# PSUM banks at sub-layer boundaries, the place of a modulation's pieces, and a shift of the weight buffers in a two-layer trunk on one core

## Chip, core and metric

The kernel runs on one core of one Trainium2 chip. The metric is the device time of one execution in microseconds. Three executions of the kernel before give a median of 1439.07 us (1438.82 to 1439.69). The engines that matter are TensorE (PE, whose weight loads are shown as PEld), VectorE (DVE), ScalarE (ACT), GpSimd (POOL) and SyncE (SP), which issues the loads of the weights.

## The reference

Two layers of a trunk of width 1024 work on 128 context tokens and 256 latent tokens. Every layer is a feed-forward network with SwiGLU, a token mixer, and another feed-forward network. Each of these six sub-layers normalises its input, scales and shifts it by vectors that come from the conditioning, and gates its output before it is added to the stream:

```python
def swiglu(h, w1, w2):
    g, u = jnp.split(h @ w1, 2, axis=-1)
    return (jax.nn.silu(g) * u) @ w2

def modulate_norm(x, g, shift, scale):
    return rms_norm(x, g) * (1.0 + scale[:, None, :]) + shift[:, None, :]
```

The mixer of the even layer is neighbourhood attention beside a gated short convolution; that of the odd layer is a pooling mixer beside grouped-query attention with rotary positions. Shift, scale and gate of each sub-layer are products of SiLU(cond) with a matrix of 1024 x 1024 each, for two conditions (context and latent). All of it is in fp32.

## The kernel before

The 384 tokens are three tiles of 128: tile 0 is context, tiles 1 and 2 are latent. The residual stream `x` stays in SBUF. A product in fp32 is made of three matmuls (`mm3`, L443 to L445): both operands are split into a high and a low part, and high x high, low x high and high x low are added in PSUM. `xh` and `xl` are the parts of the current sub-layer's normalised and modulated input, transposed. The weights come in 1 MB pieces through four `raw` buffers, loaded by SP in the order of one list (`plan`, L1309); each piece has two halves, and each half is split by ACT (cast to `whi`, L152) and DVE (subtraction to `wlo`, L155) into one of three pairs of buffers, or into special ones (`macc`, `th`, `g`).

Beside the matmuls, DVE works out the modulation vectors of later sub-layers. A modulation matrix is four pieces of work (L229): a multiply and reduce of 128 x 1024 with `csB`, the SiLU of the conditions broadcast over partitions, which GpSimd loads (L203). The product goes to a bf16 scratch `junkv` that nobody reads. `emit_pieces` puts them between other work of DVE. `spread` (L1301) says where the matrices stand among a sub-layer's weights on SP's list.

The change touches the boundary between two sub-layers. The old sub-layer's last products are accumulated tile after tile, in PSUM banks 2 and 3, 4 and 5, 6 and 7 for tiles 0, 1 and 2. While TensorE is still at work on later tiles, the earlier ones are gated, added to `x`, normalised (`xn`), transposed on TensorE into PSUM and modulated out of PSUM into `xtmp` by DVE (L414) and ACT (L416), then cast to `xh` (ACT, L429) and subtracted to `xl` (DVE, L430). For tile 2 there is nothing of the old sub-layer left to hide this. `rest(early, late)` (L541) therefore lets the new sub-layer begin on tiles 0 and 1 (`early`), puts tile 2's transposes and modulation between, and comes back to the new sub-layer's first weights for tile 2 alone (`late`). In the feed-forward network `run_t2` (L656) multiplies tile 2 with the first two units, into `pn`; `fold` (L672) transposes the finished product and splits it. In the mixers `moving_first` (L1017) does the same, with `early` looping over token tiles and, in `moving`, over the `rows` of a half (2 in the even mixer, 1 in the odd one).

Up to this point the instructions are in the order in which the code writes them. The rest of the even mixer is ordered by a scheduler. There, `q`'s products in `psB0` and `psB1` are taken from PSUM by DVE (L1080) and ACT (L1081), then attention runs between the projections.

## Time and profile before

| | |
|---|---|
| median of three runs | 1439.07 us |
| the profiled execution | 1439.5 us |
| its span | 1437.6 us |
| TensorE busy | 1417.9 us, 99% |
| DVE busy | 1021.9 us, 71% |
| ACT busy | 614.6 us, 43% |

The durations that follow are those of the one profiled execution; its span is the time from the first to the last instruction. In a timeline a row is one instruction or a run of like ones, with its start, its duration, its engine and its line of the code; in brackets stands how long the engine had been idle before, and what ended that.

### The profile page before, as it was taken

How to read it: one execution, taken by the hardware profiler on the slowest of the kernel's cores; microseconds unless marked ns; L12 is line 12 of the kernel's file. 1: busy time of each engine (PE TensorE's matmuls, PEld its weight loads, DVE VectorE, ACT ScalarE, POOL GpSimd, SP SyncE). 2: the span in 40 equal slices, each digit the busy share in tenths (PEclk: the TensorE clock that was granted, in tenths of full speed). 3: DMA queues.
4: the chain of work that ended last, by engine and by line, in shares of the span. 5: the costliest groups of instructions: out<-in, count | busy, mean ns of one | idle time of the engine just before them, and what ended most of it. 6: DMA issues, size and time to landing. Idle time of an engine off the chain costs nothing.

```text
span 1437.6 us, 19880 instructions
## 1 busy us (share of the span) xinstructions
PE 1417.9 (99%) x7747; PEld 1299.1 (90%) x7747; DVE 1021.9 (71%) x1798; ACT 614.6 (43%) x1051; POOL 29.0 (2%) x54
## 2 busy tenths in 40 slices
PE   8999999999999999999999999999999999999998
PEld 6999998879888999999889999988886899999886
DVE  5688868578997677986855889787678755555333
ACT  5533332463545633333355333323657653333232
POOL 0000000020000000000000000000100000000000
PEclk9999999999999999999999999999999999999999
DMA  9556556626545246655734566566350234444331
GB/s 371 208 212 253 202 209 224 245 104 235 200 146 195 97 169 230 237 205 182 280 124 150 202 219 249 186 226 249 108 200 30 118 118 148 165 155 176 122 113 44
DMA packets 38959, 262.59 MB, mean 183 GB/s; under 512 B 4816, under 2 KB 4976, under 8 KB 8784
## 3 DMA queue, kind: packets, MB, share of 16 engines
q1 hardware_dynamic: 35424, 243.29, 46.2%
q0 software_dynamic: 3440, 18.02, 3.4%
q8 instruction: 61, 1.00, 0.3%
q14 instruction: 34, 0.28, 0.1%
HBM read 259.01 MB, written 2.29 MB: 182 GB/s over the span
## 4 chain that ended last, share of the span: by engine, by line
PE 93%; ACT 3%; DVE 3%; DMA 1%; issue 1%; DVEq 0%; SPq 0%; ACTq 0%
PE psB L443 29%; PE psB L444 29%; PE psB L445 29%; PE psB L391 2%; PE psB L938 1%; PE psB L979 1%; ACT xtmp L416 1%; DMA csB<-crows 1%; ACT junk L331 1%; ACT xh L429 1%; PE psB L785 0%; DVE xtmp L414 0%; ACT whi L152 0%; DVE wlo L155 0%; ACT L617 0%
## 5 line engine op out<-in xcount | busy, mean ns | idle before, releaser
L443 PE MATMUL psB<-xh,whi 128*128 128x384 f32 (+1 forms) x1536 | 519.5, 338 | 2.2 <-ACT qz L1081 2.0
L444 PE MATMUL psB<-xl,whi 128*128 128x384 f32 (+1 forms) x1536 | 514.7, 335 | 0.2 <-DVE xl L430 0.2
L445 PE MATMUL psB<-xh,wlo 128*128 128x384 f32 (+1 forms) x1536 | 514.2, 335 | 0.0
L155 DVE TENSOR_TENSOR wlo<-raw,whi 128x1024 fp32r<-128x1024 f32 (+2 forms) x286 | 336.4, 1185 | 121.8 <-ACT whi L152 120.0
L152 ACT CAST whi<-raw 128x1024 fp32r<-128x1024 f32 (+1 forms) x275 | 285.7, 1045 | 309.7 <-PE psB L444 147.7
L229 DVE CUSTOM_DVE_ANT_0 junkv<-raw,csB,mbT 128x1024 bf16<-128x1024 f32 x256 | 327.9, 1281 | 9.8 <-DMA csB<-crows 5.0
L443 PEld LDWEIGHTS psB<-xh,whi 128*128 128x128 f32 x1536 | 288.5, 188 | 7.0 <-ACT qz L1081 2.3
L444 PEld LDWEIGHTS psB<-xl,whi 128*128 128x128 f32 x1536 | 288.7, 188 | 1.8 <-DVE xl L430 0.9
L445 PEld LDWEIGHTS psB<-xh,wlo 128*128 128x128 f32 x1536 | 288.7, 188 | 0.4 <-issue 0.4
L443 PE MATMUL psB<-whi,g 128*128 128x512 f32 x384 | 149.9, 390 | 0.0
L445 PE MATMUL psB<-whi,g 128*128 128x512 f32 x384 | 149.5, 389 | 0.0
L444 PE MATMUL psB<-wlo,g 128*128 128x512 f32 x384 | 149.4, 389 | 0.0
L429 ACT CAST g<-gt 128x384 fp32r<-128x384 f32 (+1 forms) x84 | 42.5, 506 | 196.7 <-DVE gt L619 196.7
L619 DVE TENSOR_TENSOR gt<-psB,sil 128x384 f32<-128x384 f32 (+1 forms) x88 | 48.1, 547 | 90.1 <-PE psB L445 81.8
L443 PEld LDWEIGHTS psB<-whi,g 128*128 128x128 f32 x384 | 72.1, 188 | 15.1
L445 PEld LDWEIGHTS psB<-whi,g 128*128 128x128 f32 x384 | 72.1, 188 | 15.1
L444 PEld LDWEIGHTS psB<-wlo,g 128*128 128x128 f32 x384 | 72.1, 188 | 14.6
L617 ACT ACTIVATE sil<-psB 128x384 f32<-128x384 f32 (+1 forms) x88 | 42.7, 485 | 90.5 <-PE psB L445 90.4
L430 DVE TENSOR_TENSOR g<-gt,g 128x384 fp32r<-128x384 f32 (+1 forms) x84 | 46.1, 549 | 48.1 <-ACT g L429 48.1
L443 PE MATMUL psB<-g,g 128*128 128x512 f32 x120 | 47.0, 391 | 0.0
L445 PE MATMUL psB<-g,g 128*128 128x512 f32 x120 | 46.8, 390 | 0.0
L444 PE MATMUL psB<-g,g 128*128 128x512 f32 x120 | 46.7, 389 | 0.0
(227 smaller groups left out, 1410.9 us busy)
## 6 DMA issues: line engine op xcount, KB each, us to landing
raw<-in_ffn_w SPq DMA_DIRECT2D x129, 1024.0 KB, 4.9
raw<-in_mod_w SPq DMA_DIRECT2D x64, 1024.0 KB, 4.9
raw<-in_ev_in SPq DMA_DIRECT2D x10, 1024.0 KB, 6.2
m<-in_mod_first SPq DMA_DIRECT2D x8, 1024.0 KB, 13.0
gate<-gscr POOLq DMA_DIRECT2D x6, 1024.0 KB, 4.9
csB<-crows POOLq DMA_DIRECT2D x4, 1024.0 KB, 7.5
raw<-in_ev_out SPq DMA_DIRECT2D x4, 1024.0 KB, 4.9
raw<-in_od_out SPq DMA_DIRECT2D x4, 1024.0 KB, 4.8
```

The costliest lines, as they stand in the source:

```text
L152: nc.scalar.copy(hi, src)
L155: sub = lambda hi=hi[:, c], lo=lo[:, c], src=src[:, c]: nc.vector.tensor_tensor(lo, src, hi.bitcast(F32), ALU.subtract)
L229: nc.vector.tensor_tensor_reduce(junk, self.raw[i][0][:, kk * D : (kk + 1) * D], self.csB[:, c, :], 1.0, self.mbT[:, s, kind, k : k + 1], ...
L331: self.nc.scalar.activation(junk, srcs[h], AF.Square, scale=1.0 / 32.0, accum_out=ss[:, h : h + 1])
L391: self.nc.tensor.transpose(out, src, self.ident)
L429: self.nc.scalar.copy(hi, src)
L430: sub = lambda: self.nc.vector.tensor_tensor(lo, src, hi.bitcast(F32), ALU.subtract)
L443: nc.tensor.matmul(out, ah, bh, start=first, stop=False)
L444: nc.tensor.matmul(out, ah, bl, start=False, stop=False)
L445: nc.tensor.matmul(out, al, bh, start=False, stop=last)
L617: nc.scalar.activation(sil[:, :n], pg[:, :n], AF.Silu)
L619: nc.vector.tensor_tensor(gt[:, :n], pu[:, :n], sil[:, :n], ALU.mult)
```

## The change

Six things change.

1. Tile 2's transposes are put into four banks, two 128-column transposes each (4, 5, 2, 3; at the odd mixer 4, 5, 6, 7), in place of two banks with four each. DVE modulates the first and third bank, ACT the second and fourth.
2. In the feed-forward networks `pn` lies in banks 4 and 3 (before 2 and 0), and the folded product's transpose in 2 and 1 (before 4 and 1).
3. In the odd mixer tile 1's accumulators lie in banks 2 and 3 (before 6 and 7); `ups` and the transposes of queries and keys that follow change banks with them.
4. In `moving_first` the loop over `kk` stands outside that over the token tiles; the transposes stand between the first and the second `kk`. With one row, as in the odd mixer, the order is the old one.
5. In the even mixer the modulation matrices begin one place later on SP's list, and the source hands out the pieces only after the third projection tile.
6. The constant `one` takes 1 column in place of 25, and `junkv` 192 bf16 elements more. Behind `one` stand `xh` and others, 96 bytes lower; behind `junkv` stand the weight buffers, 288 bytes higher. Weight buffers and `xh` are 384 bytes further apart.

```diff
--- before.py
+++ after.py
@@ -66,7 +66,7 @@
         self.cc = cc
         self.ident = const("ident", [P, P])
         make_identity(nc, self.ident)
-        self.one = const("one", [P, 25])[:, 0:1]
+        self.one = const("one", [P, 1])
         nc.vector.memset(self.one, 1.0)
         self.xh = self.cp.tile([P, KC, TOK], F32R, tag="xh", name="xh")
         self.xl = self.cp.tile([P, KC, TOK], F32R, tag="xl", name="xl")
@@ -225,9 +225,9 @@
                     if u == 0:
                         self.mod_res = self.mod_vec(kind)
                 k = 2 * u + kk
-                junk = self.cp.tile([P, D], BF16, tag="junkv", name=self.name("junkv"))
+                junk = self.cp.tile([P, D + 192], BF16, tag="junkv", name=self.name("junkv"))
                 nc.vector.tensor_tensor_reduce(
-                    junk, self.raw[i][0][:, kk * D : (kk + 1) * D], self.csB[:, c, :], 1.0,
+                    junk[:, :D], self.raw[i][0][:, kk * D : (kk + 1) * D], self.csB[:, c, :], 1.0,
                     self.mbT[:, s, kind, k : k + 1], ALU.mult, ALU.add, self.mod_res[:, c, k : k + 1])
                 if kk == c == 1:
                     del self.raw[i]
@@ -392,8 +392,9 @@
 
     def transpose_x(self, xn, banks):
         tp = [self.psum(b) for b in banks]
+        n = KC // len(tp)
         for k in range(KC):
-            self.transpose(tp[k // 4][:, (k % 4) * P : (k % 4 + 1) * P], xn[:, k * P : (k + 1) * P])
+            self.transpose(tp[k // n][:, (k % n) * P : (k % n + 1) * P], xn[:, k * P : (k + 1) * P])
         return tp
 
     def evac_steps(self, t, tp, s):
@@ -408,8 +409,9 @@
                 for j in range(2):
                     c = 2 * e + j
                     k = 4 * q + c
-                    src, scale, shift = (tp[q][:, c * P : (c + 1) * P], self.scale[s][:, cond, k : k + 1],
-                                         self.shift[s][:, cond, k : k + 1])
+                    n = KC // len(tp)
+                    src, scale, shift = (tp[k // n][:, (k % n) * P : (k % n + 1) * P],
+                                         self.scale[s][:, cond, k : k + 1], self.shift[s][:, cond, k : k + 1])
                     if e == 0:
                         nc.vector.tensor_scalar(st[q, e][:, j, :], src, scale, shift, op0=ALU.mult, op1=ALU.add)
                     else:
@@ -559,7 +561,8 @@
             for f in subs[1 + odd :]:
                 f()
             evac = []
-            transposes = lambda: evac.append(self.evac_steps(2, self.transpose_x(xn2, (4, 5)), s + 1))
+            banks = (4, 5, 6, 7) if odd else (4, 5, 2, 3)
+            transposes = lambda: evac.append(self.evac_steps(2, self.transpose_x(xn2, banks), s + 1))
             early(0)
             finish = early(1)
             if odd:
@@ -656,7 +659,7 @@
             def run_t2(n):
                 u, h = divmod(n, 2)
                 if h == 0:
-                    pn[u] = self.psum((2, 0)[u])
+                    pn[u] = self.psum((4, 3)[u])
                 for kk in range(4):
                     k = 4 * h + kk
                     c = slice(kk * 256, kk * 256 + 256)
@@ -670,7 +673,7 @@
                 return None
 
             def fold(u, gn):
-                tp = self.psum((4, 1)[u])
+                tp = self.psum((2, 1)[u])
                 self.transpose(tp[:, 0:P], gn[:, 0:P])
                 gh, gl = g_of(u)
                 self.split(gh[:, t2], gl[:, t2], tp[:, 0:P])
@@ -1005,9 +1008,9 @@
         es.close()
         return nxt
 
-    def moving(self, ps, key, h, w, rows, width, t, blocks):
-
-        for kk in range(rows):
+    def moving(self, ps, key, h, w, rows, width, t, blocks, kks=None):
+
+        for kk in range(rows) if kks is None else kks:
             k = (2 * key[1] + h) * rows + kk
             for b, (c0, c1) in enumerate(blocks):
                 c = slice(kk * width + c0, kk * width + c1)
@@ -1023,10 +1026,11 @@
         def early(n, between=None):
             k, h = halves[n]
             ws.append(self.half(k, h, ahead=0, hold=True))
-            for t in range(2):
-                if t == 1 and between:
+            for kk in range(rows):
+                if kk == 1 and between:
                     between()
-                self.moving(ps, k, h, ws[-1], rows, width, t, blocks)
+                for t in range(2):
+                    self.moving(ps, k, h, ws[-1], rows, width, t, blocks, (kk,))
 
         def late():
             ps[2] = [self.psum(b) for b in banks[2]]
@@ -1146,7 +1150,8 @@
                 ps = self.proj_tile(key, h, n % 2, step)
                 n += 1
                 evac[kind](j, ps)
-                self.emit_pieces(pieces, 2)
+                if n > 3:
+                    self.emit_pieces(pieces, 2)
         while pieces:
             self.emit_pieces(pieces, 1)
         for _ in att:
@@ -1174,7 +1179,7 @@
         nc.gpsimd.dma_start(rope, io["rope"])
         tabs = mp.tile([P, 2, 2, 2, 64], F32, tag="tabs", name="tabs")
         units = [k for k in p1 if k[0] == "od_qkv"]
-        acc = self.moving_first(units, 1, 768, [(0, 512), (512, 768)], [(0, 1), (6, 7), (4, 5)], rest)
+        acc = self.moving_first(units, 1, 768, [(0, 512), (512, 768)], [(0, 1), (2, 3), (4, 5)], rest)
         for a in range(2):
             for b in range(2):
                 nc.vector.tensor_tensor(tabs[:, a, :, b, :], rope[:, :, b, :],
@@ -1219,12 +1224,12 @@
             return raw
 
         def qk_transpose(t, raw):
-            tp = self.psum((0, 6, 4)[t])
+            tp = self.psum((0, 2, 4)[t])
             for i in range(4):
                 self.transpose(tp[:, i * P : (i + 1) * P],
                                raw[:, 2 * i : 2 * i + 2, :].rearrange("p h d -> p (h d)"))
             nc.scalar.copy(qT[:, :, t * P : (t + 1) * P], tp.rearrange("p (i q) -> p i q", i=4))
-            tk = self.psum((1, 7, 5)[t])
+            tk = self.psum((1, 3, 5)[t])
             self.transpose(tk[:, 0:P], raw[:, 8:10, :].rearrange("p h d -> p (h d)"))
             c0 = 384 if t == 0 else (t - 1) * P
             nc.vector.tensor_copy(kz[0:64, 0, c0 : c0 + P], tk[0:64, 0:P])
@@ -1233,7 +1238,7 @@
         nc.gpsimd.dma_start(pm, io["pool_m"])
         nc.gpsimd.dma_start(pw, io["pool_w"])
         nc.gpsimd.dma_start(psc, io["pool_scale"])
-        ups = [[self.psum(2)], [self.psum(3)], None]
+        ups = [[self.psum(6)], [self.psum(7)], None]
         uc = [(k, h) for k in p1 if k[0] == "od_uc" for h in range(2)]
         raws = {}
         for n, (k, h) in enumerate(uc):
@@ -1323,7 +1328,7 @@
             b2 = [("od_out", i) for i in range(4)]
         n, n1 = MOD_PLAN[s]
         ext, mods = mods[:n], mods[n:]
-        b1 = spread(b1, ext[:n1], 3 if j == 1 else 5, len(b1))
+        b1 = spread(b1, ext[:n1], 4 if j == 1 else 5, len(b1))
         phases.append((b1, spread(b2, ext[n1:], 0, 7)))
     return phases, [k for p1, p2 in phases for k in p1 + p2]
 
```

TensorE's order at the boundary into the even mixer, before (`psB0` and `psB1` are the accumulators of tiles 0 and 1, `whi_496` and `wlo_497` the last half of the first weights, `psB4` and `psB5` hold the transposes of tile 2):

```order
L443 MATMUL psB0_482_2737<-whi_496_2777,xh_92 128x512
L444 MATMUL psB0_482_2737<-wlo_497_2778,xh_92 128x512
L445 MATMUL psB0_482_2737<-whi_496_2777,xl_93 128x512
L443 MATMUL psB0_482_2737<-whi_496_2777,xh_92 128x512
L444 MATMUL psB0_482_2737<-wlo_497_2778,xh_92 128x512
L445 MATMUL psB0_482_2737<-whi_496_2777,xl_93 128x512
L391 MATMUL psB4_506_2832<-ident_85,xn_505_2798 128x128 x4
L391 MATMUL psB5_507_2833<-ident_85,xn_505_2798 128x128 x4
L443 MATMUL psB1_483_2738<-whi_496_2777,xh_92 128x512
L444 MATMUL psB1_483_2738<-wlo_497_2778,xh_92 128x512
```

and after:

```order
L445 MATMUL psB0_482_2737<-whi_496_2777,xh_92 128x512
L446 MATMUL psB0_482_2737<-wlo_497_2778,xh_92 128x512
L447 MATMUL psB0_482_2737<-whi_496_2777,xl_93 128x512
L445 MATMUL psB1_483_2738<-whi_496_2777,xh_92 128x512
L446 MATMUL psB1_483_2738<-wlo_497_2778,xh_92 128x512
L447 MATMUL psB1_483_2738<-whi_496_2777,xl_93 128x512
L391 MATMUL psB4_506_2832<-ident_85,xn_505_2798 128x128 x2
L391 MATMUL psB5_507_2833<-ident_85,xn_505_2798 128x128 x2
L391 MATMUL psB2_508_2834<-ident_85,xn_505_2798 128x128 x2
L391 MATMUL psB3_509_2835<-ident_85,xn_505_2798 128x128 x2
L445 MATMUL psB0_482_2737<-whi_496_2777,xh_92 128x512
L446 MATMUL psB0_482_2737<-wlo_497_2778,xh_92 128x512
```

The second `kk` of tile 0, which needs the second half of `wlo`, has moved behind the transposes, and those have four banks.

TensorE's order in sub-layer 2, from the first two weights' products for tile 2 to the third's, before:

```order
L445 MATMUL psB2_921_4627<-macc_834_4228,xl_93 128x256
L443 MATMUL psB2_921_4627<-macc_834_4228,xh_92 128x256
L444 MATMUL psB2_921_4627<-macc_834_4228,xh_92 128x256
L445 MATMUL psB2_921_4627<-macc_834_4228,xl_93 128x256
L443 MATMUL psB0_925_4659<-whi_896_4484,xh_92 128x256
L444 MATMUL psB0_925_4659<-wlo_897_4485,xh_92 128x256
```

and after:

```order
L447 MATMUL psB4_925_4631<-macc_836_4230,xl_93 128x256
L445 MATMUL psB4_925_4631<-macc_836_4230,xh_92 128x256
L446 MATMUL psB4_925_4631<-macc_836_4230,xh_92 128x256
L447 MATMUL psB4_925_4631<-macc_836_4230,xl_93 128x256
L445 MATMUL psB3_929_4663<-whi_898_4486,xh_92 128x256
L446 MATMUL psB3_929_4663<-wlo_899_4487,xh_92 128x256
```

The order is the same; the second accumulator of tile 2 is bank 3 in place of bank 0, and the first one bank 4 in place of bank 2.

DVE's order in the even mixer, from the first copy of `v` to the first `q`, before (L1076 copies `v`, L229 are the modulation's pieces, L155 is a weight's low part, L1080 takes `q` out of `psB0`):

```order
L1076 COPY v_2729<-psB0_482_2737 128x512
L229 ISA junkv_534_3026,mv_533_3025<-raw_429_2471,csB_522_2928,mbT_77 128x1024
L229 ISA mv_533_3025 128x1
L1076 COPY v_2729<-psB7_515_2874 128x512
L155 TENSOR_TENSOR wlo_524_2931<-raw_433_2510,whi_523_2930 128x1024
L229 ISA junkv_535_3028,mv_533_3025<-raw_429_2471,csB_522_2928,mbT_77 128x1024
L229 ISA mv_533_3025 128x1
L229 ISA junkv_540_3063,mv_533_3025<-raw_429_2471,csB_522_2928,mbT_77 128x1024
L229 ISA mv_533_3025 128x1
L1080 TENSOR_SCALAR qz_2727<-psB0_525_2934 64x384
```

and after (four lines of code are added above, so that L1076 is L1080 and L1080 is L1084):

```order
L1080 COPY v_2729<-psB0_482_2737 128x512
L229 ISA junkv_543_3092,mv_542_3091<-raw_433_2510,csB_524_2930,mbT_77 128x1024
L229 ISA mv_542_3091 128x1
L1080 COPY v_2729<-psB7_517_2876 128x512
L155 TENSOR_TENSOR wlo_526_2933<-raw_429_2471,whi_525_2932 128x1024
L229 ISA junkv_544_3094,mv_542_3091<-raw_433_2510,csB_524_2930,mbT_77 128x1024
L229 ISA mv_542_3091 128x1
L229 ISA junkv_549_3129,mv_542_3091<-raw_433_2510,csB_524_2930,mbT_77 128x1024
L229 ISA mv_542_3091 128x1
L1084 TENSOR_SCALAR qz_2727<-psB0_527_2936 64x384
```

The pieces stand at the same places; they read `raw_433` in place of `raw_429`, and the weight's low part reads `raw_429`.

## Rows read from the trace of the kernel before

**Rows 1.** the page, part 1 (busy us, share of the span, instructions)

```profile
PE 1417.9 (99%) x7747; PEld 1299.1 (90%) x7747; DVE 1021.9 (71%) x1798; ACT 614.6 (43%) x1051; POOL 29.0 (2%) x54
```

**Rows 2.** TensorE's waits by releaser: us in total, times, longest us

```profile
PE psB L443 <- ACT sil L617: 2.8, 3, 1.0
...
PE psB L443 <- ACT xh L429: 0.9, 5, 0.2
```

**Rows 3.** timeline into sub-layer 2 (start, us, engine, line; [idle before <-releaser])

```profile
482.61 0.81 ACT L416 ACTIVATE xtmp<-psB,mv,mv 128x128 f32<-128x128 f32 x2 [1.97 <-DVE xtmp L414]
...
483.32 0.28 PE L445 MATMUL psB<-xh,wlo 128*128 128x256 f32 x1
...
483.76 0.39 PE L443 MATMUL psB<-whi,xh 128*128 128x256 f32 x1 [0.16 <-ACT xh L429]
...
486.78 0.28 PE L445 MATMUL psB<-macc,xl 128*128 128x256 f32 x1
...
487.58 0.38 ACT L617 ACTIVATE sil<-psB 128x256 f32<-128x256 f32 x1
...
488.02 0.38 PE L443 MATMUL psB<-whi,xh 128*128 128x256 f32 x1 [0.96 <-ACT sil L617]
```

**Rows 4.** the same timeline: the product that is folded, its transpose

```profile
490.99 0.28 DVE L668 TENSOR_TENSOR sil<-psB,sil 128x128 f32<-128x128 f32 x1
...
492.27 0.27 PE L391 MATMUL psB<-ident,sil 128*128 128x128 f32 x1
```

**Rows 5.** timeline at the boundary into the even mixer, TensorE

```profile
310.76 0.40 PE L443 MATMUL psB<-whi,xh 128*128 128x512 f32 x1
...
311.61 0.50 PE L444 MATMUL psB<-wlo,xh 128*128 128x512 f32 x1 [0.46 <-DVE wlo L155]
```

**Rows 6.** timeline at the boundary into the odd mixer

```profile
1035.93 0.28 PE L445 MATMUL psB<-whi,xl 128*128 128x256 f32 x1
...
1037.19 0.47 PE L443 MATMUL psB<-whi,xh 128*128 128x512 f32 x1 [0.98 <-DVE ry L314]
...
1041.08 0.72 ACT L385 ACTIVATE xn<-x,rz 128x512 f32<-128x512 f32 x1 [0.68 <-DVE rz L322]
...
1041.08 0.49 DVE L384 TENSOR_SCALAR xn<-x,rz 128x512 f32<-128x512 f32 x1
...
1042.50 1.03 PE L391 MATMUL psB<-ident,xn 128*128 128x128 f32 x8
```

**Rows 7.** timeline in the even mixer, where TensorE waits longest

```profile
327.16 1.28 DVE L229 CUSTOM_DVE_ANT_0 junkv<-raw,csB,mbT 128x1024 bf16<-128x1024 f32 x1 [4.96 <-DMA csB<-crows]
...
331.42 0.34 PE L445 MATMUL psB<-xh,wlo 128*128 128x384 f32 x1
...
332.64 0.54 DVE L1080 TENSOR_SCALAR qz<-psB 64x384 f32<-64x384 f32 x1
...
333.76 0.45 PE L443 MATMUL psB<-xh,whi 128*128 128x384 f32 x1 [2.00 <-ACT qz L1081]
```

**Rows 8.** a window after it: busy us of five engines, granted clock

```profile
334.90:338.40 3.50, 3.50 (x13) 3.50 (x12) 3.46 (x7) 0.48 (x1) 0.00 (x0) 0.51 0.83 297
```

**Rows 9.** windows of four streams: us, TensorE's busy us (matmuls), granted clock

```profile
60.00:110.00 50.00, 50.00 (x285) 1.00 0.53 189
...
115.00:165.00 50.00, 50.00 (x291) 1.00 0.63 229
...
565.00:615.00 50.00, 50.00 (x288) 1.00 0.66 232
...
830.00:905.00 75.00, 75.00 (x427) 1.00 0.63 229
```

**Rows 10.** groups by form: 384-column matmuls of one of three lines

```profile
L443 PE MATMUL psB<-xh,whi 128*128 128x384 f32 x1464 | 499.1, 341 | 2.2 <-ACT qz L1081 2.0 <-ACT xh L429 0.2
```

**Rows 11.** timeline at the even mixer's end, DVE and TensorE

```profile
442.59 6.90 DVE L155 TENSOR_TENSOR th<-raw,th 128x1024 fp32r<-128x1024 f32 x6 [0.40 <-ACT th L152]
...
445.03 0.39 PE L443 MATMUL psB<-th,mh 128*128 128x512 f32 x1
```


## The prediction

> **What bounds the kernel now.** Read the page's first part: TensorE is busy for 1417.9 us, 99% of the span, DVE for 71% and ACT for 43% [rows 1]. So work saved on another engine is worth only what TensorE waits for it, and the second thing to read is the list of TensorE's waits. Two entries recur at the boundaries: three waits of about 1.0 us for ACT's `sil` and five of about 0.2 us for `xh` [rows 2]. The timeline shows how they arise. At a boundary the third tile's transposes lie in two banks; DVE and ACT share each bank, and ACT's modulation stood idle for 1.97 us behind DVE's [rows 3]. Everything that ACT does afterwards in order (the casts of `xh`, the next weight cast, `sil`) is late by that. The granted clock is 1.00 in the streams [rows 9], and half in a stretch of the even mixer, after the longest wait there [rows 7, 8]. What is left is pace: how far apart two matmuls start when nothing is waited for [rows 9].
>
> **The step that I use.** A window of 50 us holds 285 matmuls of 384 columns, of which some two reach over its ends, so one starts every 50/283 = 176.7 ns, or 0.46 ns a column [rows 9]: 0.12 us for 256 columns and 0.23 us for 512, as estimates.
>
> **The `sil` waits (FFN boundaries, three times).** TensorE's next matmul starts at 488.02 after one at 486.78, 1.24 us for a step of 0.12, so 1.12 us are lost [rows 3]. It waits because `pn[1]` lies in bank 0, which holds the accumulator that ACT's `sil` reads first. Three such waits have 2.8 us of idle [rows 2], with the slower restart (some 0.15 each) 3.3 us. After the change `pn[1]` is bank 3, whose last reader is ACT's modulation, done before 486.8 even in the old order; the wait goes. What is late next is the fold: its product (L668) ends at 490.99 + 0.28 = 491.27, and TensorE took its transpose at 492.27 [rows 4]. TensorE now comes there 1.12 + 0.32 us earlier, at 490.83. Had the product not moved, 0.44 us would be waited for; ACT's chain moves forward by about 0.8 us, because its first modulation no longer stands behind DVE's two in the same bank (482.61 becomes about 481.8, if two of DVE's take as long as the 0.81 us that two of ACT's take), and with it the product ends near 490.5. I take 0.1 us each, bounds 0 and 0.44. Net 3.3 - 0.3 = **3.0 us**.
>
> **The `xh` waits (all five boundaries).** A step from 483.32 to 483.76 is 0.44 us, 0.32 more than 0.12, of which 0.16 is listed as idle [rows 3]. Five waits with 0.9 us of idle [rows 2] and as much again of restart make 1.7 us. With ACT's chain 0.8 us earlier, TensorE finds `xh` ready even where it itself comes earlier by 0.4. At the even boundary it comes earlier by 0.6, which still leaves 0.2. I take **1.6 us**.
>
> **The even boundary.** From 310.76 to 311.61 is 0.85 us for a step of 0.23: 0.62 us for the second half of `wlo` [rows 5]. With `kk` as the outer loop both token tiles use the first half, and then the transposes stand, before the second half is wanted: two matmul groups and eight transposes of cover where there was none. The transposes then stand 0.6 us earlier and need `xn2`, whose producers run at that very time; a few tenths could come back. **0.6 us**, bounds 0.2 and 0.8.
>
> **The odd boundary.** From 1035.93 to 1037.19 is 1.26 us, 1.14 over the step: tile 1's second block wants banks 6 and 7, which DVE still reads as the sub-layer's last accumulators [rows 6]. With (2, 3) it doesn't wait. But the next consumer of that same chain is near: the transposes of `xn2` ran at 1042.50, and `xn2` is written by DVE until 1041.57 and by ACT until 1041.80. TensorE would be there at 1041.36. Its new wait is between 0.2 (DVE's half, taken by the first four transposes) and 0.45; with 0.35, 1.14 becomes **0.8 us**.
>
> **Four banks for the transposes, by themselves** add nothing to TensorE: eight transposes before and after. DVE and ACT modulate the same columns; only the banks part them.
>
> **The even mixer's modulation.** The three-tile delay in the source should take DVE's multiply-reduces (L229, 1.28 us) out of the way of `q`'s evacuation: at 327.16 the first waited 4.96 us for `csB`, behind it stand the copy, a weight subtract and two more, and L1080 reached `psB0` at 332.64. TensorE stood from 331.42 to 333.76, 2.34 us for a step of 0.18: 2.16 us lost [rows 7]. But this part of the program is ordered by the scheduler, and DVE's order there is the same after the change, row for row; only which raw buffer is read differs. `csB`'s transfer is the same too. So I take **0**. Some 1.2 us after TensorE resumes, the granted clock is 0.51 for 3.5 us, the lower of its two levels (1.2 GHz) instead of 2.4 [rows 8], in which 13 matmuls run instead of some 20; the lost 7 steps are about 1.3 us. If the wait goes, 2.16 + 1.3 = 3.5 us go with it: that is this part's lower bound. On the other side, the modulation matrix and the input weights change places on SP's queue, so that each later matrix lands one transfer later, and the last one's reduces move to the end of the mixer, ahead of the subtracts of `th`: those start at 442.59, one takes 1.15, and TensorE takes the first at 445.03, with 1.3 us to spare [rows 11]. Two of the reduces that move there would be 2.6 us, a wait of 1.3. Bounds: 3.5 us less to 1.5 us more.
>
> **The addresses.** The constant of 25 columns becomes 1, and the bf16 scratch grows by 384 bytes, so all weight buffers stand 384 bytes further from `xh`. No instruction is added. What may move is the pace: at a granted clock of 1.00 four windows of the same kind of matmul have 283, 289 and 286 in 50 us and 425 in 75 us, that is 176.7, 173.0, 174.8 and 176.5 ns [rows 9]. The paces belong to whole stretches and no wait explains them. There are 3 x 1464 = 4392 such matmuls [rows 10], so a nanosecond is 4.4 us. With about half of them at the slow pace the mean is near 175.4; all at 173.0 would be 10.5 us less, all at 176.7 5.7 us more. I find no row that ties the pace to a distance between buffers, and take 0.
>
> The Trainium skill's page "TensorE: Matmul & The Clock Gate" (section "Wait — 56ns, not 53.3ns?") gives N / 2.4 GHz plus about 2.5 ns from start to start, whatever the addresses. For 384 columns that would be 162.5 ns, as an estimate from it, one pace for all, and the address part would be worth nothing. The windows disagree: none is so fast, and they differ among themselves.
>
> **The sum.** 3.0 + 1.6 + 0.6 + 0.8 = 6.0 us off the profiled execution's 1439.5, which is 0.4 above the median of 1439.07, inside the spread of the runs. From the median: **1433.0 us**. The bounds of the small terms (folds, transposes of `xn2`, modulation at the mixer's end) make 1429 to 1436 of it.
>
> **Rivals.**
> - *Pace better*: the changed distance or the removed waits put more streams at 173 to 174 ns. For it: the same instructions run at both paces in this trace [rows 9]. Against it: no row shows a distance at work. Half of the 10.5 us gives 1428, all of it 1422.5.
> - *Pace worse, not slower*: streams that are at 173.0 or 174.8 fall to 176.7. 1433.0 + 5.7 = 1438.7, no change that can be told.
> - *Pace worse than any seen (slower than before)*: the distance disturbs TensorE's reading of moving and weight data in all the 384-column streams. A further step as large as those between the windows is 178.5 ns; (178.5 - 175.4) x 4392 = 13.6 us, so 1446.6. It outweighs the gain of 6.0 from a mean of 176.8 ns on, and is slower by 0.2% from 177.4, which no window shows.
> - *The modulation does come later in effect* (the wait at 331 goes, and the half clock): 1429.5. The order of DVE speaks against it.
> - *The waits move instead of going*: `csB`, folds, transposes and the mixer's end take back 4 us. 1437, for it that each consumer found above is within half a microsecond.
>
> **How the numbers follow.** My sum 0.50; pace better 0.16; modulation 0.07; waits moved or pace worse within the old paces 0.17; slower 0.10. A measurement here can tell 0.2%, 2.9 us, from no change. Faster by more: 0.50 + 0.16 + 0.07 and a small part of the moved waits, 0.75; within: 0.15; slower: 0.10. The range leaves out the best pace below and the slower case above: 1426 to 1439.5.
>
> **What would show it.** Right: no `sil` wait at the FFN boundaries and TensorE's waits for `xh` gone; at the odd boundary a short wait on `xn` before the transposes; ACT's first modulation of tile 2 beginning with DVE's. The wait at `qz` still about 2 us, with half the clock after it. Wrong: a changed count of matmuls in windows of 50 us without any wait, which is the address part, or new waits on `gn`, on modulation matrices or on `th`.

## The result

The changed kernel takes 1422.67 us (median of 4 runs, 1422.17 to 1423.91) beside 1439.2 of the kernel before; the ratio is 0.9886, interval 0.9869 to 0.9903. I had said 1433.0 and a range down to 1426.0: the direction was right, the size was not. The profiled execution has a span of 1421.0 us, 16.6 less.

The table takes the same matmul of the three split-product lines in both traces and subtracts its start times; the steps between its lines show where the time went.

```
matmul  place                                before    after   difference
   500  sub-layer 0, first streams            116.5    115.2     -1.2
  1475  before the even boundary              309.8    308.7     -1.1
  1495  after it                              316.5    314.2     -2.3
  1590  after the wait for qz, half clock     338.6    333.4     -5.2
  1760  after the first attention             371.5    368.1     -3.4
  2215  before the boundary into sub-layer 2  482.8    479.0     -3.9
  2300  after it                              495.2    489.6     -5.6
  3715  before the boundary into sub-layer 3  763.0    755.4     -7.6
  3800  after it                              775.4    766.0     -9.4
  5150  before the odd boundary              1035.5   1023.3    -12.2
  5400  in the odd mixer's output product    1125.6   1113.4    -12.1
  5575  before the boundary into sub-layer 5 1160.7   1148.5    -12.2
  5660  after it                             1173.0   1159.1    -13.9
  7007  last                                 1430.6   1413.9    -16.7
```

The boundaries give 1.2 + 1.7 + 1.8 + 1.7 = 6.4 us, and the odd one nothing: close to the 6.0 of the forecast, but partly by luck, since one part came out larger and another at nothing. The even mixer keeps 1.1 (2.9 won, 1.8 given back). Some 9 us more are won at no one place: they come evenly inside the streams, where nothing is waited for. The windows of the changed kernel (us, TensorE's busy us and matmuls, granted clock, DMA share, GB/s) that answer to [rows 9]:

```profile
60.00:110.00 50.00, 50.00 (x290) 1.00 0.54 191
...
115.00:165.00 50.00, 50.00 (x291) 1.00 0.63 233
...
565.00:615.00 50.00, 50.00 (x290) 1.00 0.62 225
...
830.00:900.00 70.00, 70.00 (x406) 1.00 0.66 236
```

All streams now hold 288 matmuls that start in 50 us (290 less the two that reach over the ends), 173.6 ns each; 285, 288 and 427 of the kernel before have become 290, 290 and, in 70 us instead of 75, 406 (173.3 ns instead of 176.5).

TensorE's waits in the changed kernel, which answer to [rows 2] (total, times, longest):

```profile
PE psB L391 <- DVE p L917: 1.2, 1, 1.2
...
PE psB L445 <- ACT qz L1085: 0.7, 1, 0.7
...
PE psB L446 <- DVE ss L337: 0.4, 1, 0.4
...
PE psB L446 <- DVE wlo L155: 0.3, 1, 0.3
...
PE psB L445 <- ACT xh L431: 0.2, 1, 0.2
```

The three waits for `sil` are gone, and one of five for `xh` is left; those at the even and the odd boundary [rows 5, 6] are gone too. New are one of 1.2 us for `p` before its transposes, one of 0.7 for `qz` in place of 2.0, and two for weights' low parts (one of them named after a neighbour, L337).

The boundary into sub-layer 2, to be held against [rows 3, 4]: ACT's modulation, its `sil`, DVE's product, and TensorE's transpose of it.

```profile
477.93 0.81 ACT L418 ACTIVATE xtmp<-psB,mv,mv 128x128 f32<-128x128 f32 x2 [1.10 <-PE psB L391]
...
482.91 0.39 ACT L620 ACTIVATE sil<-psB 128x256 f32<-128x256 f32 x1
...
486.32 0.28 DVE L671 TENSOR_TENSOR sil<-psB,sil 128x128 f32<-128x128 f32 x1
...
486.66 0.33 PE L391 MATMUL psB<-ident,sil 128*128 128x128 f32 x1
```

ACT begins its modulation 1.10 us after its last work, when TensorE has made the transposes, and no longer 1.97 behind DVE. The product ends at 486.60 and the transpose starts at 486.66: the fold is what TensorE meets next, as forecast. It loses 0.18 us there.

### The profile page after: what moved, and what is told of

Read it like the earlier page. It is cut to its first block, busy times and chain, and to the rows that moved or that the text cites. A ratio compares the mean times of both kernels' runs of the same rounds, so it can differ in the third digit from the quotient of the medians.

```text
span 1421.0 us, 19853 instructions
## 1 busy us (share of the span) xinstructions
PE 1405.4 (99%) x7747; PEld 1287.3 (91%) x7747; DVE 1021.1 (72%) x1798; ACT 614.5 (43%) x1051; POOL 29.0 (2%) x54
## 4 chain that ended last, share of the span: by engine, by line
PE 93%; DVE 3%; DMA 1%; ACT 1%; issue 1%; DVEq 0%; SPq 0%; ACTq 0%; POOLq 0%
PE psB L445 29%; PE psB L446 29%; PE psB L447 29%; PE psB L391 2%; PE psB L941 1%; PE psB L982 1%; DVE junkv L229 1%; DVE wlo L155 1%; DMA raw<-in_mod_w 1%; DMA csB<-crows 1%; PE psB L788 0%; ACT junk L331 0%; DMA x<-in_x_prompt 0%; PE psB L955 0%; PE psB L801 0%
## 5 line engine op out<-in xcount | busy, mean ns | idle before, releaser
L155 DVE TENSOR_TENSOR wlo<-raw,whi 128x1024 fp32r<-128x1024 f32 (+2 forms) x286 | 336.6, 1186 | 121.0 <-ACT whi L152 119.2
L229 DVE CUSTOM_DVE_ANT_0 junkv<-raw,csB,mbT 128x1024 bf16<-128x1024 f32 x256 | 328.1, 1281 | 8.8 <-DMA csB<-crows 3.7
```

The lines of the kernel that those rows point to most:

```text
L155: sub = lambda hi=hi[:, c], lo=lo[:, c], src=src[:, c]: nc.vector.tensor_tensor(lo, src, hi.bitcast(F32), ALU.subtract)
L229: nc.vector.tensor_tensor_reduce(junk[:, :D], self.raw[i][0][:, kk * D : (kk + 1) * D], self.csB[:, c, :], 1.0, self.mbT[:, s, kind, k : k ...
```

## The experiments

Unless it is said otherwise they start from the kernel before, so that one part stands alone. A kernel's time is the median of its runs. Beside these kernels the kernel before took 1432.6 to 1439.9 (median 1436.79 of 16 runs beside the first four), and not the narrow 1438.8 to 1439.7 of the forecast's runs; why it can spread is part of the answer below. That it did not on every chip (six of the seven runs beside the last two kernels took 1438.9 to 1439.8) is not explained by any run. "By the starts" means, as in the table above, that the start of the same matmul in two traces is subtracted.

**What moves the pace.** Four kernels:

```diff
addr_only, junk_only (with the first pair or without)
-        self.one = const("one", [P, 25])[:, 0:1]
+        self.one = const("one", [P, 1])
-                junk = self.cp.tile([P, D], BF16, tag="junkv", name=self.name("junkv"))
+                junk = self.cp.tile([P, D + 192], BF16, tag="junkv", name=self.name("junkv"))
```

`one_only` has the first pair alone; `no_addr` is the changed kernel with both undone.

> The kernel before with nothing but the address part: `one` takes 1 column, `junkv` 192 elements more. Theory A (the pace depends on where the buffers lie): all 384-column streams go at about 173.3 ns, the waits of the kernel before stay, so about 9.5 us less than before, 1429.6. Theory B (the pace went up because the waits at the boundaries went): no change, 1439.

> The changed kernel with the addresses of the kernel before. Theory A: the streams are back at 173.0 to 176.7 ns, some 9.5 us above the changed kernel, 1432.2, near the forecast without a change of pace. Theory B: 1422.7 as the changed kernel.

> The kernel before with only `one` at 1 column: `xh` and the weight buffers lie 96 bytes lower together. Theory A1 (their distance matters): no change, 1439. Theory A2 (each buffer's own address matters, say in units of 64 bytes, of which 96 is no multiple): the whole 9.5 us, 1429.6.

> The kernel before with only `junkv` 192 elements longer: `xh` stays, the weight buffers lie 384 bytes higher. Theory A1 (distance): 1429.6. Theory A2 (own address in units of 64 bytes, of which 384 is a multiple): no change, 1439.

Measured: addr_only 1429.86 (1429.38 to 1430.33; ratio 0.9948, 0.9929 to 0.9966), no_addr 1429.68 (1427.69 to 1430.59), one_only 1438.83 (1438.37 to 1439.43), junk_only 1429.84 (1429.57 to 1430.18). Theory B falls: without any change at a boundary the whole effect is there, 9.2 us against the forecast's median of 1439.07 and 6.9 against that chip's. So does A2: `xh` and weights moved together win nothing. It is the distance between what lies before `junkv` and what lies behind it. That `xh` and the weights are the pair that matters is concluded, not isolated, since other buffers behind `junkv` move with them; but a matmul of these streams reads nothing else, and the 512-column products of `whi` with `g`, both behind `junkv`, keep a mean step of 226.8 to 226.9 ns in all these traces. One thing in one_only stays open: its eight runs lie within 1.1 us at the slow end, while eight of the 16 of the kernel before took less than 1437. The windows of no_addr show what the old distance does:

```profile
60.00:110.00 50.00, 50.00 (x285) 1.00 0.53 189
...
115.00:165.00 50.00, 50.00 (x291) 1.00 0.64 228
...
565.00:615.00 50.00, 50.00 (x291) 1.00 0.66 236
...
830.00:880.00 50.00, 50.00 (x285) 1.00 0.65 226
```

Two streams are fast and two slow, and not the same as in the trace of before, where the third was at 174.8. At the old distance a stream falls into one of several paces. I take it that this also changes from execution to execution, and that it is the spread of 7 us of the kernel before and the reason why no_addr came out 2.5 below what I expected; no kernel was traced twice, so this is not shown directly. With 384 bytes more every stream is at the best of them.

**Which distances.** `junkv` longer by 64, 128, 256, 32 and 96 elements, as above, with `one` as before. The distances in the table are worked out from the sizes of the buffers; no trace shows addresses.

> The kernel before with `junkv` 64 elements longer: weight buffers 128 bytes further from `xh` in place of 384, distance 448 modulo 512 (before 320, the 384 case 192). Theory A1a (the bad case is one narrow value, or a distance that is near a multiple of 256): at 192 modulo 256 as in the 384 case, steady 173.3 ns, 1429.8. Theory A1b (only 384 bytes by themselves are good, with a period of 512 or more): paces between 173 and 177 as before, 1433 to 1439.

> The same with 128 elements: 256 bytes further, 64 modulo 512 and the same as before modulo 256. If the period is 256 bytes, as slow and changing as before, 1433 to 1439; if it is 512 or more, this may be fast, 1429.8.

> The same with 256 elements: 512 bytes further, 320 modulo 512 as before. If the distance counts modulo 512 (or a divisor of it), as slow and changing as before, 1433 to 1439; if a larger distance is better by itself, 1429.8.

> The kernel before with `junkv` 32 elements longer: weight buffers 64 bytes further from `xh`, a distance of 128 modulo 256 (before 64). Theory C1 (64 modulo 256 is the exception): steady 173.3 ns, 1429.8. Theory C2 (192 is the exception): paces that change between 173 and 177, 1433 to 1439.

> The same with 96 elements: 192 bytes further, 0 modulo 256. Theory C1: steady 173.3 ns, 1429.8. Theory C2: 1433 to 1439. A third case: where both buffers begin at the same place modulo 256 the pace is worst of all, 176.7 or above in every stream, 1441 or more.

```
bytes added   distance mod 256   us, median (lowest to highest)
0 (before)          64           1436.79 (1432.58 to 1439.46)
64                 128           1441.60 (1440.78 to 1442.22)
128                192           1430.39 (1429.60 to 1430.83)
192                  0           1431.18 (1430.82 to 1431.44)
256                 64           1435.99 (1434.39 to 1439.53)
384                192           1429.84 (1429.57 to 1430.18)
512                 64           1436.91 (1432.68 to 1439.25)
```

The rows of 64 and 192 bytes more were taken on another chip than the rest, beside 1437.51 (1434.24 to 1439.73) of the kernel before. The distance counts modulo 256 bytes, as far as these seven show. 64 is slow and changing, 128 slow and steady, 192 and 0 fast and steady: C1 and C2 both fall, since neither one is the only exception. The third case of dist_192, that an equal place modulo 256 is worst, falls too. The windows of dist_64 (32 elements), then of dist_256 (128), then the first of dist_192 (96):

```profile
60.00:110.00 50.00, 50.00 (x286) 1.00 0.54 190
...
115.00:165.00 50.00, 50.00 (x287) 1.00 0.63 227
...
565.00:615.00 50.00, 50.00 (x286) 1.00 0.65 227
```

```profile
60.00:110.00 50.00, 50.00 (x284) 1.00 0.53 191
...
115.00:165.00 50.00, 50.00 (x291) 1.00 0.62 230
...
565.00:615.00 50.00, 50.00 (x288) 1.00 0.65 231
```

```profile
60.00:110.00 50.00, 50.00 (x291) 1.00 0.53 194
```

At 128 all streams hold 284 to 285 starts, 176 ns; at 64 they differ, as before. dist_192 is as fast as 384 bytes in the streams; the 1.3 us that it is behind junk_only stand at the three FFN boundaries, in the 256-column products, some 0.4 us at each by the starts.

**What the boundary parts are worth.** These have the address part too, so that the pace is steady, and are held against addr_only's 1429.86.

```diff
addr_pn
-                    pn[u] = self.psum((2, 0)[u])
+                    pn[u] = self.psum((4, 3)[u])
-                tp = self.psum((4, 1)[u])
+                tp = self.psum((2, 1)[u])
addr_banks4 (and transpose_x and evac_steps as in the change)
-            transposes = lambda: evac.append(self.evac_steps(2, self.transpose_x(xn2, (4, 5)), s + 1))
+            transposes = lambda: evac.append(self.evac_steps(2, self.transpose_x(xn2, (4, 5) if odd else (4, 5, 2, 3)), s + 1))
```

> The address part and, beside it, only the banks of `pn` and of the folded product; the transposes of tile 2 stay in two banks. To be held against the kernel with the address part alone (1429.86). My theory: the three `sil` waits of 2.8 us go, but the product that is folded isn't earlier, so TensorE waits some 0.1 to 0.4 us for it at each FFN boundary; the `xh` waits stay. About 2.7 us less, 1427.2. Rival (the wait only moves on to the folded product): less than 1 us is left, 1429.

> The address part and, beside it, only the four banks of tile 2's transposes (at the odd mixer they stay in two, as its accumulators do). Against the address part alone (1429.86). My theory: ACT's first modulation begins with DVE's, its whole chain comes 0.8 us earlier; the `xh` waits at four boundaries go (some 0.3 us each), and the `sil` waits shrink by 0.8 less what TensorE itself comes earlier, to about 0.5 each. Some 1.2 + 1.5 = 2.7 us less, 1427.2. Rival (the two parts of the FFN boundary are worth something only together): under 1.3 us less.

addr_pn: 1427.62, 2.2 less; by the starts, 0.8 to 1.0 at each of the three FFN boundaries. (That makes 2.7 or 2.8; the total is less because its trace loses 0.7 in the even mixer, where the wait for `qz` is 1.9 us, with the half clock after it, in place of 1.3 without.) Its waits:

```profile
PE psB L443 <- ACT xh L429: 0.9, 5, 0.2
...
PE psB L391 <- DVE sil L668: 0.5, 3, 0.2
```

No wait for `sil` is left, three of 0.2 for the product that is folded. The rival falls. addr_banks4: 1425.60, 4.3 less, more than the 2.7 expected, and otherwise made up. Its waits:

```profile
PE psB L445 <- ACT sil L619: 2.4, 3, 0.8
...
PE psB L445 <- ACT xh L431: 0.2, 1, 0.2
```

The `xh` waits go (one is left), 0.65 at each FFN boundary by the starts and 0.8 to 1.0 with what `sil` adds, since the slow restart goes with them. But the `sil` waits hardly shrink, from 2.8 to 2.4: TensorE comes earlier by nearly what ACT does. The even boundary gives 0.4, about as expected. The rest comes from a place that I hadn't named: 0.7 at `qz`, where `csB` arrives earlier. In addr_only its load is issued by GpSimd 0.20 us ahead of SP's next 1 MB; DVE's first reduce shows when it is there (SPq is SP's queue of issues):

```profile
317.21 0.53 POOL L203 DMA_DIRECT2D csB<-crows  x1 [7.72 <-ACT whi L152]
...
317.41 0.33 SPq L119 DMA_DIRECT2D raw<-in_mod_w  x1
...
325.32 1.28 DVE L229 CUSTOM_DVE_ANT_0 junkv<-raw,csB,mbT 128x1024 bf16<-128x1024 f32 x1 [4.32 <-DMA csB<-crows]
```

In addr_banks4 the two issues stand the other way round:

```profile
316.38 0.33 SPq L119 DMA_DIRECT2D raw<-in_mod_w  x1
...
316.57 0.54 POOL L203 DMA_DIRECT2D csB<-crows  x1 [7.32 <-ACT whi L152]
...
324.02 1.28 DVE L229 CUSTOM_DVE_ANT_0 junkv<-raw,csB,mbT 128x1024 bf16<-128x1024 f32 x1 [3.66 <-DMA csB<-crows]
```

From issue to first use it is 8.1 us there and 7.5 here; the 0.66 between them is what `qz` gains. The other traces go the same way: from issue to landing the load takes 8.1 to 8.7 us in all eleven with GpSimd 0.2 us first, 7.1 to 7.4 in the six with SP 0.2 us ahead (the changed kernel's among them). No run tells why.

**The even mixer's modulation.**

```diff
addr_mod
-                self.emit_pieces(pieces, 2)
+                if n > 3:
+                    self.emit_pieces(pieces, 2)
-        b1 = spread(b1, ext[:n1], 3 if j == 1 else 5, len(b1))
+        b1 = spread(b1, ext[:n1], 4 if j == 1 else 5, len(b1))
late_order (from the changed kernel: order_end() no longer ahead of the loop)
                 evac[kind](j, ps)
-                if n > 3:
+                if n == 4:
+                    self.order_end()
+                if n > 4:
                     self.emit_pieces(pieces, 2)
```

> The address part and, beside it, only the even mixer's modulation (list one place later, pieces after the third tile). Against the address part alone. My theory: DVE's order up to the attention is the same, so TensorE's wait for `qz` stays between 1.3 and 2.2 us, and what it changes by comes back in the wait for `p` before its transposes some 30 us later; 1429.9, within 0.5. Rival (the later list makes `csB` land earlier and that is kept): 1.3 us less, 1428.5.

> The changed kernel, with the scheduler taking over only after the even mixer's fourth projection tile, so that DVE takes `q` out of its bank before the modulation's pieces, which the change meant and the scheduler undid. My theory: the 0.85 us wait for `qz` goes, but the pieces fill DVE all the same, so the wait for `p` grows by as much: 1422.7, within 0.5. Rival (the first wait is gained outright): 1421.8 or less.

addr_mod: 1429.23 (1429.22 to 1429.82), within what the runs spread: this part of the change, on its own, is worth nothing that can be told. late_order: 1421.95 (two runs) against 1422.67. The wait for `qz` is gone, and by the starts TensorE is 1.0 ahead there and 1.8 once the attention has ended; then it gives 0.9 back, most of it in a wait for `th`, which DVE now prepares later:

```profile
PE psB L391 <- DVE p L917: 0.9, 1, 0.9
...
PE psB L446 <- DVE th L155: 0.6, 1, 0.6
```

My theory, that the wait for `p` grows by as much, was wrong: it shrank from 1.2 to 0.9, and 0.85 stays by the starts. That is nearer the rival, although 0.7 us between medians of two and four runs, from different sets, is little.

**The odd mixer's banks.** The changed kernel with the four edits at the odd mixer undone (and the transposes in two banks):

> The changed kernel with the odd mixer's banks as before (accumulators of tile 1 in 6 and 7, transposes in 4 and 5). Against the changed kernel (1422.67). My theory: the wait of 1.14 us at tile 1's block is back, and the two waits of 0.6 us for the weights' low parts, which the changed kernel has instead, are gone: 1422.7, within 0.3. Rival (my forecast): 0.8 us slower, 1423.5.

1422.90 against 1422.67: nothing that can be told, as the theory said. By the starts, the old wait costs 1.2 at its place, and 1.2 comes back within 8 us; 0.3 is lost again a little later.

**Less work for DVE in the even mixer.** From the changed kernel, the number of modulation matrices under sub-layer 0 and under the even mixer, and how many of them lie under the first product:

```diff
-    (16, 11), (8, 8), (17, 12), (19, 14), (0, 0), (4, 4),
plan18, plan18_late
+    (18, 12), (6, 6), (17, 12), (19, 14), (0, 0), (4, 4),
plan18b
+    (18, 13), (6, 6), (17, 12), (19, 14), (0, 0), (4, 4),
plan17
+    (17, 12), (7, 7), (17, 12), (19, 14), (0, 0), (4, 4),
```

> The changed kernel with 18 modulation matrices in the first sub-layer and 6 in the even mixer (before 16 and 8): 8 pieces of 1.28 us, 10.3 us of DVE's work, move to the first sub-layer. Theory D1 (DVE's load sets the even mixer's waits): the 1.65 us wait for `p` goes and most of the one for `qz`, about 2 us less than the changed kernel, 1420.7. Theory D2 (the waits are set by when `csB` lands and by the order): 1422.7. Rival (the first sub-layer has no room, and loads of weights come late there): 1424 or more.

> The same with the scheduler taking over after the fourth projection tile, as in late_order. D1: both waits go, and the new ones at the mixer's end too: 1420.0. D2: as late_order, 1421.9.

> As plan18 (two modulation matrices out of the even mixer), but 13 of the first sub-layer's 18 lie under its first product, so that its second product has 5 as in the changed kernel. D1 (DVE's load bounds the mixer): the 6.5 us that plan18 lost in the second product don't arise, the 1.6 us that it gained in the mixer stay: 1421.1. Rival (the first product has no room either): 1424 or more.

> One matrix moved (12 of 17 under the first product), and the scheduler takes over after the fourth projection tile, as in late_order (1421.95). D1: half of plan18's 1.6 us, on top of late_order: 1421.1. D2 (only the order counts): 1421.95.

plan18: 1430.01, plan18_late 1429.12. A sixth matrix under sub-layer 0's second product makes weights late there, and 8 us are lost between 233 and 262:

```profile
PE psB L446 <- DVE wlo L155: 2.6, 4, 0.8
...
PE psB L445 <- ACT whi L152: 2.4, 2, 1.5
```

These waits are 5.0 us; for 3.4 us from 250.3 the granted clock was 0.50 besides. plan18b has five there, as the changed kernel, and comes to 1421.53 (1421.17 to 1421.83), the lowest of all; it is 1.1 below the changed kernel's median, which is from another set of runs, and by the starts 1.5 are gained in the mixer. plan17 came to 1422.25 (1422.12 to 1423.16), where D1 expected 1421.1. plan17, against late_order's 1421.95, shows nothing won by its one matrix. Two matrices win something: in plan18 and plan18b alike TensorE gains some 1.1 us by the starts at one place, near the attention's end (423 to 430), so less load on DVE helps in the mixer's second half; the wait for `p` at the first attention stayed, 1.6 and 1.5 us. How the order and the load share in it is not shown.

## Why the prediction was wrong

**The addresses** are the step that failed: "I find no row that ties the pace to a distance between buffers, and take 0." The forecast was 10.3 us too high; the addresses alone are worth 9.2 against the forecast's median, and 7 beside the kernel before on the same chip (addr_only). The rows had the effect's size (the rival with all streams at 173.0 comes to 1422.5, against 1422.67 measured; so close by luck, since the streams gave 9.2 and not 10.5, and the even mixer 1.1 that the sum didn't have) but not its cause, and I gave it a part of 0.16. What the trace did show, three paces for like streams at one clock and with no wait, was the sign that something in the operands' reading was in an unlucky state; a change that moves just those operands should have had a larger chance, on both sides: 64 bytes more put all streams at some 176 ns and are 2 to 5 us slower. That is the rival whose streams fall to 176.7, for which I had 5.7; no window shows a pace beyond it, for which I had 13.6.

The Trainium skill's page "SBUF — State Buffer" (section "Who interferes with whom") says that TensorE has one read port for the moving operand and another, independent one for the weights, and waits on nobody. By that the distance should not count. The measurement differs and decides: with nothing changed but the length of `junkv`, 1429.84 or 1441.60. How the distance acts, by the two reads meeting or otherwise, is not shown by any run.

**`sil`.** Forecast 3.0; addr_pn gives 2.7 or 2.8 by the starts, with 0.2 each given to the fold where I took 0.1. Right.

**`xh`.** Forecast 1.6 at five boundaries. At the FFN boundaries both parts together give 1.7 each, of which 0.9 is `sil`'s; so the earlier `xh` gives 0.8 (0.65 directly, in addr_banks4), more than twice the 0.3 that I took, because the slow restarts after it went too. The mechanism was right, the term too small.

**The even boundary.** 1.2, for 0.6 and 0.3 as its share of `xh`: the mechanism was right, the size somewhat small.

**The odd boundary.** Forecast 0.8, measured 0. I had looked for the next consumer and found `xn2`; nearer ones were the low parts of the second weights' two halves, which wait for the same chain of DVE and ACT. The short wait on `xn` that I had named as a sign didn't come: TensorE, late by the first of these waits, found it ready. The rows of after:

```profile
1027.00 0.40 PE L445 MATMUL psB<-whi,xh 128*128 128x512 f32 x1
...
1027.81 0.50 PE L446 MATMUL psB<-wlo,xh 128*128 128x512 f32 x1 [0.42 <-DVE ss L337]
...
1030.37 0.96 DVE L155 TENSOR_TENSOR wlo<-raw,whi 128x768 fp32r<-128x768 f32 x1 [0.99 <-ACT whi L152]
...
1030.57 0.47 PE L445 MATMUL psB<-whi,xh 128*128 128x512 f32 x1
...
1031.38 0.50 PE L446 MATMUL psB<-wlo,xh 128*128 128x512 f32 x1 [0.34 <-DVE wlo L155]
```

1027.00 to 1027.81 and 1030.57 to 1031.38 are 0.81 each for steps of 0.23. Together that is 1.16, all of the 1.14 that was won. Before the first, DVE went from one instruction to the next without a gap. Before the second it stood idle itself, 0.99 us, for ACT's cast, which comes behind ACT's half of `xn`. That chain of DVE and ACT is the bound here, whatever TensorE's banks are; old_odd shows the same.

**The modulation.** Forecast 0 with a lower bound of 3.5 less. The part itself is worth 0 (addr_mod), but "`csB`'s transfer is the same too" failed: from issue to first use it took 8.74 us before and 7.46 after. The wait shrank from 2.16 to 0.85, and the sign that I had named, some 2 us with half the clock after it, didn't come:

```profile
323.55 1.29 DVE L229 CUSTOM_DVE_ANT_0 junkv<-raw,csB,mbT 128x1024 bf16<-128x1024 f32 x1 [3.67 <-DMA csB<-crows]
...
329.12 0.34 PE L447 MATMUL psB<-xh,wlo 128*128 128x384 f32 x1
...
330.15 0.44 PE L445 MATMUL psB<-xh,whi 128*128 128x384 f32 x1 [0.69 <-ACT qz L1085]
...
365.13 0.74 DVE L917 TENSOR_SCALAR p<-p,r 128x384 f32<-128x384 f32 x2
...
365.59 0.55 PE L391 MATMUL psB<-ident,p 128*128 128x128 f32 x3 [1.16 <-DVE p L917]
```

DVE begins its reduces 3.6 us earlier than before, of which TensorE's own lead is 2.3 and the shorter load 1.3, and `q` is out of its bank that much earlier. No half clock followed; nor did one in addr_only, whose wait is 1.3. But from there DVE has hardly a gap (0.4 us, for a modulation matrix) until `p` is scaled at 365.13, and TensorE, now ahead, waits for it: 1.65 us from one matmul's start to the next there, 1.16 of it idle by the profile. Of the 2.9 us won at 330 to 338, 1.8 were given back at 366. Here a wait that was taken away came up again, in part, at the next product of a supplier that had no room.

**The rival "the waits move"** took place in these two spots, inside the sum.

## What to carry to other kernels

Where like matmuls run at several paces at one granted clock and with no wait, try the distance between the buffers that they read before hunting for waits of a tenth as much: a pad of a few hundred bytes is a cheap trial, and here it was worth 7 to 9 us, more than all the banks together (6.4). When a wait is removed, list what the same supplier makes next, and for whom; the odd boundary and the attention gave back all and more than half. An order that the source sets by emission can be undone by a scheduler: compare the order, not the source.

## What the hardware showed that was not expected

The pace of 384-column matmuls with weights of 128 columns depends on the distance of the two operands modulo 256 bytes: 173 ns at 192 and 0, 176 at 128, and 173 to 177 from stream to stream at 64. Matmuls of another form need not follow: those of 512 columns with `whi` moving and `xh` as weights took 229 to 230 ns on average at 64 and at 0, but 233 at 128 and 192 (kernels without the boundary parts, pauses left out). So a pad is to be chosen for the form that has most of the time.

The half clock after the wait for `qz` doesn't follow from the wait's length alone: it came in the traces of before (idle 2.0 us), of addr_pn (1.9) and of dist_64 (1.7), and not in those of dist_256 (2.0), junk_only, addr_mod and dist_128 (1.7 each).
